# A decoder block's first MLP operands made all through the attention, loads issued further ahead at changes of stage, and w_down's sums spread over five products

## The chip, the cores and the metric

The kernel runs as one program on one core of a Trainium2 chip. The metric is the device time of one execution in microseconds (us). The profile speaks of TensorE (PE, and PEld for its weight loads), VectorE (DVE), ScalarE (ACT), GpSimd (POOL) and SyncE (SP). Two engines issue transfers here: SP, whose queue shows as SPq, and POOL. Each queue is worked off in order, so an entry that waits holds what stands behind it.

## What is computed

One layer over 2048 tokens of width 1024. The reference, cut to what matters here:

```python
h = rms_norm(x, pre_norm_mix) * (1 + sc_a) + sh_a
y = hybrid_mixer(h, ...)          # GLA heads and differential attention, concatenated, @ w_out
x = x + gt_a * rms_norm(y, post_norm_mix)

h = rms_norm(x, pre_norm_mlp) * (1 + sc_m) + sh_m
y = jnp.square(jax.nn.relu(h @ w_up)) @ w_down     # 1024 -> 4096 -> 1024
x = x + gt_m * rms_norm(y, post_norm_mlp)
```

`diff_attention` is causal, two softmax maps for each of 4 heads, with (p1 - lam * p2) @ v. All values are f32.

## The kernel before

A product of f32 accuracy is made of three matmuls: each operand is split into a high part (rounded by a copy on ACT) and a low part (the rest, a subtraction on DVE), and high*high, high*low and low*high are summed in PSUM. So an operand passes through a load, ACT and DVE before PE can use it.

The stages stand one after the other in the program: modulation and projections with GLA; attention over the first 1024 tokens (`attention((0, 1), ...)`, here A0), then over the second 1024 (A1), with the product by w_out (`out_proj`) run as filler between their steps; the rest of `out_proj`; w_up; w_down. A scheduler sets the order of instructions on each engine from the order of the code and its own model, and tiles come from pools with a fixed number of buffers, so that a load waits until the last reader of its buffer is through.

**Attention.** For a query block of 128 and a key chunk of 512, `qk` makes the scores S (PE) and moves them to SBUF with a running minimum (DVE, L214 and L217); `softmax` does the exponentials (ACT, L227) and joins the two maps (DVE, L233); two steps later `pv` transposes P (PT, PE L248), copies it out (PTs, ACT L250) and multiplies with V (O, PE L252); `finish` normalises a head's output (`don` on DVE, its transposes `dps` on PE) and stores it in `mixS`.

**out_proj.** For one token tile (128 tokens) it loads `mx` from `mixS` and `xt` from x, makes 48 matmuls (Y, L873 to L875) in 16 resumptions, adds the result to x (`wxt`, on POOL for tiles below 11), stores it in `x1S`, and stores the row-normalised tile in `xnS`. `interleave` resumes it between attention steps, as soon as the heads of a tile are finished (`ready`). Tiles 0 to 10 are done so, in this order; tiles 11 to 15 after the attention.

**First operands of w_up.** `prep_first` takes the normalised rows of the first 1024 tokens back from `xnS` (`xnq`), transposes them (`ntr`), modulates them (`hBq`, ACT), forms four differences (`hTq`, DVE) and stores seven operands in `hS[0]`. It does so in 16 groups, once 132 resumptions of `out_proj` are through, that is late in A1. Its loads are on SP's queue, its stores on POOL's.

**MLP.** w_up and w_down are 2x2 block products by the Strassen-Winograd scheme, seven products each (numbered 1 to 7, with operand slots `OP`). In w_up, for each half g of the tokens' operands and each pair of column tiles, the order of products is `WORD = (1, 6, 5, 2, 7, 3, 4)`; an operand `hhi`, `hlo` of the tokens is loaded and split by `load_op` two steps (one product of two weight tiles, 24 matmuls) before its use. Results go through `up_out` into seven sums `uS`. In w_down the order is `DORD = (1, 2, 6, 7, 4, 5, 3)`, 16 steps p each; `down_ops` loads one `us` (512 KB) and one weight tile and splits both, two steps ahead (`AHEAD`). `down_w` makes the weights' sums: in product 1 the blocks a21 + a22 - a11, stored in `wdS[p][0]`; in product 2 it loads that back and stores a12 minus it in `wdS[p][1]`; products 6 and 3 load those, 7 and 5 make a sum each. At the end, `final` adds a token tile to the residual and stores it; `load_x1` fetches that residual into four buffers.

Of the kernel before, what the change touches and what calls it, by code (L numbers as in the profile page):

```python
# [19 lines left out]
P = 128  # L20
S = 2048
D = 1024
# [27 lines left out]
def tile_hybrid_block(  # L50
# [851 lines left out]
    wdS = [dram.tile([P, 2, 512], F32, name=f"wdS{p}") for p in range(NP_)]  # L902


    def prep_first(pool, tag):


        for i in range(4):
            for k in range(4):
                raw = pool.tile([P, 2, 2, P], F32, tag="prq", name="xnq", bufs=2)  # L910
                for j in range(2):
                    nc.sync.dma_start(raw[:, j], xnS[0][:, 4 * j + i].rearrange("p (e k) c -> p e k c", e=2)[:, :, k, :])
                ps = pp.tile([P, 2, 2, P], F32, tag=tag, name="ntr", bufs=2)
                yield
                for e in range(2):
                    for j in range(2):
                        nc.tensor.transpose(ps[:, e, j, :], raw[:, j, e, :], ident)
                bt = pool.tile([P, 2, 2, P], F32, tag="prq", name="hBq", bufs=2)
                for e in range(2):
                    kk = k + 4 * e  # L920
                    nc.scalar.activation(bt[:, e], ps[:, e], AF.Identity, bias=cols[:, 24 + kk:25 + kk],
                                         scale=prem[:, 1, kk:kk + 1])
                tt = pool.tile([P, 4, P], F32, tag="prq", name="hTq", bufs=2)
                cs = slice(P * i, P * i + P)
                b4 = bt.rearrange("p i j c -> p (i j) c")
                nc.vector.tensor_tensor(tt[:, 0:2], bt[:, :, 1, :], b4[:, 0:2], op=ALU.subtract)
                nc.vector.tensor_tensor(tt[:, 2], b4[:, 3], tt[:, 0], op=ALU.subtract)
                nc.vector.tensor_tensor(tt[:, 3], b4[:, 2], tt[:, 2], op=ALU.subtract)
                nc.gpsimd.dma_start(hS[0][:, 0, k, cs], b4[:, 0])
                nc.gpsimd.dma_start(hS[0][:, 1:3, k, cs], b4[:, 2:4])  # L930
                nc.gpsimd.dma_start(hS[0][:, 3:7, k, cs], tt)
                yield
# [3 lines left out]
    op = out_proj(range(TB))  # L936

    def interleave(at, first, rate, later, pre=None):
# [3 lines left out]
        while run(at, 1):  # L942
            due += rate if i < first else later
            while due >= 1.0:
                if len(wsteps) == 16 * TB or not ready(len(wsteps) // 16):
# [34 lines left out]

    c2 = ExitStack()
# [33 lines left out]
    def load_op(g, i, pool):  # L1015

        hi = pool.tile([P, 4, 512], F32R, tag=f"hhi{i}", name="hhi", bufs=1)
        lo = pool.tile([P, 4, 512], F32R, tag=f"hlo{i}", name="hlo", bufs=1)
        for kp in range(2):
            ks = slice(2 * kp, 2 * kp + 2)  # L1020
            src = prep_tile("hsrc", [P, 2, 512])
            nc.sync.dma_start(src, hS[g][:, OP[i], ks, :])
# [41 lines left out]
    WORD = (1, 6, 5, 2, 7, 3, 4)  # L1064
# [3 lines left out]
    op = out_proj(range(TB, 16))  # L1068
    run(op, 2)
    load_op(0, 1, sh)  # L1070
    run(op, 14)
    for p in range(2):
        for w in BLOCKS:
            load_w1(p, w)
            run(op, 4)
        sums_w(p)
    run(op, 8)
# [61 lines left out]
    n = len(usteps)  # L1139
    prep_todo = [(k, hf) for k in range(4) for hf in range(2)]  # L1140
    for s, (g, c, wi, p) in enumerate(usteps):
        i = WORD[wi]
        if s + 2 < n:
            g2, c2_, wi2, p2 = usteps[s + 2]
# [22 lines left out]
        if g == 0 and c >= 1 and wi in (2, 5) and p % 2 == 0 and prep_todo:  # L1167
            prep_step(1, *prep_todo.pop(0), pp, (("ntr", 1), ("ntr", 1)))
    assert not prep_todo
# [18 lines left out]
    def wd_sum(p, at):  # L1188
        t = sd.tile([P, 512], F32, tag="wds", name="wds", bufs=4)
        nc.sync.dma_start(t, wdS[p][:, at, :])  # L1190
        return t

    def down_w(i, p):

        if i == 1:
            wt = wd_block(p, 0, 0)
            a21, a22 = wd_block(p, 0, 1, "wdx"), wd_block(p, 1, 1, "wdx")
            nc.vector.tensor_tensor(a21, a21, a22, op=ALU.add)
            nc.vector.tensor_tensor(a21, a21, wt, op=ALU.subtract)
            nc.gpsimd.dma_start(wdS[p][:, 0, :], a21)  # L1200
        elif i == 2:
            wt = wd_block(p, 1, 0)
            s2 = sd.tile([P, 512], F32, tag="wdx", name="wdx", bufs=4)
            nc.sync.dma_start(s2, wdS[p][:, 0, :])
            nc.vector.tensor_tensor(s2, wt, s2, op=ALU.subtract)
            nc.gpsimd.dma_start(wdS[p][:, 1, :], s2)
        elif i in (6, 3):
            wt = wd_sum(p, 0 if i == 6 else 1)
        elif i == 7:
            wt, a21 = wd_block(p, 0, 0), wd_block(p, 0, 1, "wdx")  # L1210
# [233 lines left out]
```

## Time and profile before

| | before |
|---|---|
| time, median of 3 executions (lowest to highest) | 2688.37 us (2684.86 to 2694.07) |
| profiled execution, its own time / span of the profile | 2693.08 us / 2691.4 us |
| PE busy, share of span | 2508.6 us, 93% |
| DVE / ACT / POOL busy | 60% / 43% / 15% |
| bytes moved | 485.08 MB, mean 180 GB/s |

The span is the profiled part of one execution; its own time has 1.7 us around it. Idle time of an engine that isn't the bottleneck costs nothing, so what counts is where PE is not at work, and for what. The stages lie in the span as follows: everything ahead of `out_proj` up to 853 us, the change from A0 to A1 at 896 to 920, A1 to about 1340, the rest of `out_proj` to 1381, w_up to 2033, w_down from 2043 to the end.

### The profile page before, as it was taken

To read this page: it belongs to the slowest core of one execution; us is meant where nothing else is said; L and a number is where in the kernel's file an instruction comes from. 1 tells how busy PE (TensorE), PEld (TensorE's weight loads), DVE (VectorE), ACT (ScalarE), POOL (GpSimd) and SP (SyncE) were. 2 spreads that over 40 slices of the span, in tenths; PEclk is the share of its full clock that TensorE was granted. 3 is DMA by queue.
4 is the path that set the end of the run, shared out by engine and by line. 5 is a ranking of instruction groups with operands and counts; after the bars stand their busy time and mean duration, and the time that the engine had idled before them with its cause. 6 is when DMAs were issued, how large, how long until landed. Compare 5 with 4: busy or idle time off the path is not lost.

```text
span 2691.4 us, 35441 instructions
## 1 busy us (share of the span) xinstructions
PE 2508.6 (93%) x12532; PEld 2058.0 (76%) x12532; DVE 1605.8 (60%) x3126; ACT 1159.0 (43%) x2185; POOL 403.3 (15%) x594
## 2 busy tenths in 40 slices
PE   3999999999998999988889999999998899999998
PEld 2887787877796788766668888788886678888886
DVE  5545855247865586767358666866665444543756
ACT  3352224312555465555436455645443324232444
POOL 1211322103311101123102222122111100000000
PEclk8999999999998999999889999999999999999999
DMA  6354551345635654555367564645337874654855
GB/s 230 103 197 132 188 184 58 131 130 191 216 126 182 207 175 166 165 175 182 128 228 236 189 232 161 207 149 172 127 128 260 296 259 143 189 167 158 269 182 193
DMA packets 224346, 485.08 MB, mean 180 GB/s; under 512 B 25456, under 2 KB 87712, under 8 KB 222624
## 3 DMA queue, kind: packets, MB, share of 16 engines
q1 hardware_dynamic: 178768, 331.17, 39.0%
q0 software_dynamic: 45392, 151.56, 15.3%
q8 instruction: 101, 1.65, 0.3%
q14 instruction: 85, 0.70, 0.1%
HBM read 327.43 MB, written 155.20 MB: 179 GB/s over the span
## 4 chain that ended last, share of the span: by engine, by line
PE 45%; issue 12%; DVE 4%; DMA 3%; POOL 3%; ACT 1%; SPq 0%; POOLq 0%; DVEq 0%; ACTq 0%
PE dn L1310 6%; PE dn L1309 6%; PE dn L1308 6%; PE upY L1163 3%; PE upY L1164 3%; PE upY L1165 3%; PE S L209 2%; PE upV L1165 2%; PE upV L1163 2%; PE upV L1164 2%; PE O L252 2%; PE upX L1163 2%; PE upX L1165 2%; PE upX L1164 2%; PE PT L248 1%
## 5 line engine op out<-in xcount | busy, mean ns | idle before, releaser
L1310 PE MATMUL dn<-dnhi,ulo 128*128 128x512 f32 x896 | 352.9, 394 | 13.2 <-DVE ulo L1235 13.1
L1308 PE MATMUL dn<-dnhi,uhi 128*128 128x512 f32 x896 | 352.2, 393 | 13.1 <-ACT dnhi L1232 10.2
L1309 PE MATMUL dn<-dnlo,uhi 128*128 128x512 f32 x896 | 351.8, 393 | 0.2 <-DVE dnlo L1234 0.2
L1233 ACT CAST uhi<-us 128x1024 fp32r<-128x1024 f32 (+1 forms) x128 | 120.7, 945 | 343.6 <-PE dn L1309 289.2
L1235 DVE TENSOR_TENSOR ulo<-us,uhi 128x1024 fp32r<-128x1024 f32 (+1 forms) x128 | 139.4, 1089 | 163.8 <-ACT uhi L1233 163.4
L1310 PEld LDWEIGHTS dn<-dnhi,ulo 128*128 128x128 f32 x896 | 169.8, 190 | 51.5 <-DVE ulo L1235 15.7
L1308 PEld LDWEIGHTS dn<-dnhi,uhi 128*128 128x128 f32 x896 | 170.0, 190 | 50.4 <-ACT dnhi L1232 10.8
L488 PE MATMUL projt<-hThi,whi 128*128 128x512 f32 x512 | 207.2, 405 | 0.6 <-DVE cols L370 0.3
L489 PE MATMUL projt<-hTlo,whi 128*128 128x512 f32 x512 | 206.6, 403 | 0.0
L490 PE MATMUL projt<-hThi,wlo 128*128 128x512 f32 x512 | 202.1, 395 | 2.1 <-DVE wlo L425 2.1
L209 PE MATMUL S<-K,q 128*128 128x512 f32 (+3 forms) x640 | 192.3, 394 | 11.2 <-DVE P L214 7.2
L1309 PEld LDWEIGHTS dn<-dnlo,uhi 128*128 128x128 f32 x896 | 170.0, 190 | 37.1 <-DVE dnlo L1234 1.0
L227 ACT ACTIVATE P<-P,nm 128x128 f32<-128x128 f32 (+15 forms) x128 | 153.7, 1202 | 63.6 <-DVE nm L217 62.9
L1055 ACT CAST wuhi<-wA 128x512 fp32r<-128x512 f32 x160 | 99.0, 619 | 167.2 <-PE upV L1164 71.9
L252 PE MATMUL O<-V,PTs 128*128 128x128 f32 x1088 | 157.2, 289 | 11.4 <-ACT PTs L250 7.3
L252 PEld LDWEIGHTS O<-V,PTs 128*128 128x128 f32 x1088 | 139.2, 197 | 35.4 <-ACT PTs L250 28.2
L1163 PE MATMUL upY<-hhi,wuhi 128*128 128x512 f32 x384 | 153.4, 400 | 11.3 <-ACT hhi L1023 11.2
L1165 PE MATMUL upY<-hhi,wulo 128*128 128x512 f32 x384 | 153.4, 399 | 2.0 <-DVE wulo L1056 2.0
L1164 PE MATMUL upY<-hlo,wuhi 128*128 128x512 f32 x384 | 153.4, 399 | 0.0
L502 PE MATMUL projn<-whi,hThi 128*128 128x256 f32 x512 | 149.1, 291 | 4.1 <-DVE cols L370 2.6
L503 PE MATMUL projn<-wlo,hThi 128*128 128x256 f32 x512 | 148.3, 290 | 0.0
L504 PE MATMUL projn<-whi,hTlo 128*128 128x256 f32 x512 | 146.8, 287 | 0.0
(309 smaller groups left out, 5684.9 us busy)
## 6 DMA issues: line engine op xcount, KB each, us to landing
us<-uS SPq DMA_DIRECT2D x96, 512.0 KB, 4.2
wA<-in_w_up_dram SPq DMA_DIRECT2D x128, 256.0 KB, 3.0
uS<-t POOLq DMA_DIRECT2D x128, 256.0 KB, 3.0
adaraw<-in_ada_w_dram SPq DMA_DIRECT2D x48, 512.0 KB, 4.3
wraw<-in_w_in_dram SPq DMA_DIRECT2D x48, 512.0 KB, 4.5
uS<-c POOLq DMA_DIRECT2D x96, 256.0 KB, 3.0
K<-kS SPq DMA_DIRECT2D x40, 512.0 KB, 4.7
wds<-in_w_down_dram SPq DMA_DIRECT2D x80, 256.0 KB, 4.5
```

What stands on the lines that cost most here:

```text
L209: nc.tensor.matmul(ps[:, :wd], qt[:, m, hl, qs], Kc[ci][:, m, :wd], start=(hl == 0), stop=(hl == 1))
L227: nc.scalar.activation(Ps[m][:, :width], Ps[m][:, :width], AF.Exp, scale=-1.0, bias=nms[m][:, t:t + 1], accum_out=sums[:, 0, m:m + 1])
L252: nc.tensor.matmul(outs[t, h][:, j, :], pt[:, kb % 4, :], Vc[g][:, kb % 4, :], start=(kb == 0), stop=(kb == nb - 1))
L488: nc.tensor.matmul(ps, whi[k][:, cs], hi[:, k, :], start=(k == 0), stop=False)
L489: nc.tensor.matmul(ps, whi[k][:, cs], lo[:, k, :], start=False, stop=False)
L490: nc.tensor.matmul(ps, wlo[k][:, cs], hi[:, k, :], start=False, stop=(k == NK - 1))
L1163: nc.tensor.matmul(ps, whi[:, k, :], hi[:, k, :], start=(first and k == 0), stop=False, skip_group_check=not first)
L1164: nc.tensor.matmul(ps, whi[:, k, :], lo[:, k, :], start=False, stop=False, skip_group_check=not first)
L1165: nc.tensor.matmul(ps, wlo[:, k, :], hi[:, k, :], start=False, stop=(k == 3), skip_group_check=not first)
L1308: nc.tensor.matmul(banks[t], uhi[:, tk], whi, start=first, stop=False, skip_group_check=on)
L1309: nc.tensor.matmul(banks[t], uhi[:, tk], wlo, start=False, stop=False, skip_group_check=on)
L1310: nc.tensor.matmul(banks[t], ulo[:, tk], whi, start=False, stop=last, skip_group_check=on)
```

## The change

- `out_proj` works through the first eight token tiles in the order 0, 4, 1, 5, 2, 6, 3, 7 (`TOKS`), since one group of `prep_first` needs tiles i and i + 4.
- `prep_first` runs from the start of the attention's second half: group n begins when the tiles that it needs are through. Its loads are on POOL's queue in place of SP's and are issued three attention yields ahead of the transposes (one before), with two yields behind a group.
- `load_op` is parted into `fetch_op` (loads) and `split_op` (ACT and DVE), three and two products ahead. The operands of products 1 and 6 lie in a pool of their own (`sq`), and those of products 1, 6 and 5 no longer wait for `out_proj`'s pool. The second token half's first operands are fetched and split in the last round of the first half.
- The operands of w_down's first two steps are loaded and split inside w_up's last round, into buffers of `sq`.
- `down_w` forms other sums at other places: a11 - a21 in product 1 or 2 (by p), a22 minus it in product 6, a12 minus that for two p in every second step of products 7 and 4, a21 + a22 in product 5. There are four subtractions or additions for each p where there were five, three stored sums where there were two. The number of matmuls stays.
- The residual has three buffers, not four, and the last tile's final sum and store come in two halves.

```diff
+    TOKS = (0, 4, 1, 5, 2, 6, 3, 7) + tuple(range(8, 16))
     def prep_first(pool, tag):
-        for i in range(4):
-            for k in range(4):
-                raw = pool.tile([P, 2, 2, P], F32, tag="prq", name="xnq", bufs=2)
-                for j in range(2):
-                    nc.sync.dma_start(raw[:, j], xnS[0][:, 4 * j + i]...[:, :, k, :])
-                ps = pp.tile([P, 2, 2, P], F32, tag=tag, name="ntr", bufs=2)
+        for n in range(16):
+            i, k = n // 4, n % 4
+            while len(wsteps) < 32 * (i + 1) + 4:
+                yield
+            raw = pool.tile([P, 2, 2, P], F32, tag="prq", name="xnq", bufs=2)
+            for j in range(2):
+                nc.gpsimd.dma_start(raw[:, j], xnS[0][:, 4 * j + i]...[:, :, k, :])
+            for _ in range(3):
+                yield
+            ps = pp.tile([P, 2, 2, P], F32, tag=tag, name="ntr", bufs=2)
...
+            for _ in range(2):
                 yield
...
-    op = out_proj(range(TB))
+    op = out_proj(TOKS[:TB])
...
-            if pre is not None and len(wsteps) >= 132:
+            if pre is not None:
                 run(pre, 1)
...
-    def load_op(g, i, pool):
-        hi = pool.tile([P, 4, 512], F32R, tag=f"hhi{i}", name="hhi", bufs=1)
-        lo = pool.tile([P, 4, 512], F32R, tag=f"hlo{i}", name="hlo", bufs=1)
+    def fetch_op(m):
+        g, i = opseq[m]
+        hsrc[m] = [prep_tile("hsrc", [P, 2, 512]) for _ in range(2)]
         for kp in range(2):
+            nc.sync.dma_start(hsrc[m][kp], hS[g][:, OP[i], 2 * kp:2 * kp + 2, :])
+    def split_op(m):
+        g, i = opseq[m]
+        ph, pl = {1: (sq, sq), 6: (sq, sh), 5: (sh, sh)}.get(i) or (sm, sm)
...
-            if c2_ == 0 and p2 % 2 == 0 and (g2, wi2) != (0, 0):
-                load_op(g2, WORD[wi2], sh if WORD[wi2] == 1 else sm)
+        if p % 2 == 0:
+            m = 7 * g + wi if c == 0 else (wi if c == NP_ // 2 - 1 and g == 0 else None)
+            for ahead, f in ((2, split_op), (3, fetch_op)):
+                if m is not None and m + ahead < 14 and (m + ahead >= 7 * (g + 1)) == (c > 0):
+                    f(m + ahead)
...
+        if (g, c, wi, p) == (1, NP_ // 2 - 1, 3, NP_ - 1):
+            wr = prep_tile("wr", [P, 2, 512])
+            ur = [prep_tile("ur", [P, 2, 512]) for _ in range(2)]
+            for d in range(2):
+                nc.sync.dma_start(ur[d], uS[d][:, OP[1]])
+                nc.sync.dma_start(wr[:, d], w_down[2 * d * P:2 * d * P + P, 0:512])
...
+        if (g, c, wi) == (1, NP_ // 2 - 1, 5):
+            d = p % 2
...
+            ready_ops[d] = (uq[:, 0:1024], uq[:, 1024:2048], wq[:, 2 * d, :], wq[:, 2 * d + 1, :])
...
     def down_w(i, p):
-        if i == 1:
-            wt = wd_block(p, 0, 0)
-            a21, a22 = wd_block(p, 0, 1, "wdx"), wd_block(p, 1, 1, "wdx")
-            nc.vector.tensor_tensor(a21, a21, a22, op=ALU.add)
-            nc.vector.tensor_tensor(a21, a21, wt, op=ALU.subtract)
-            nc.gpsimd.dma_start(wdS[p][:, 0, :], a21)
-        elif i == 2:
-            wt = wd_block(p, 1, 0)
-            s2 = sd.tile([P, 512], F32, tag="wdx", name="wdx", bufs=4)
-            nc.sync.dma_start(s2, wdS[p][:, 0, :])
-            nc.vector.tensor_tensor(s2, wt, s2, op=ALU.subtract)
-            nc.gpsimd.dma_start(wdS[p][:, 1, :], s2)
-        elif i in (6, 3):
-            wt = wd_sum(p, 0 if i == 6 else 1)
+        if i in (1, 2):
+            wt = wd_block(p, i - 1, 0)
+            if (i == 1) == (p % 2 == 1 and p > 1):
+                a11 = wt if i == 1 else wd_block(p, 0, 0, "wdx")
+                a21 = wd_block(p, 0, 1, "wdx")
+                nc.vector.tensor_tensor(a21, a11, a21, op=ALU.subtract)
+                wd_store(p, 0, a21)
+        elif i == 6:
+            wt, s3 = wd_block(p, 1, 1), wd_sum(p, 0, "wdx")
+            nc.vector.tensor_tensor(s3, wt, s3, op=ALU.subtract)
+            wd_store(p, 1, s3)
+            wt = s3
+        elif i in (7, 4):
+            wt = wd_sum(p, 0) if i == 7 else wd_block(p, 1, 1)
+            if p % 2 == 0:
+                q = p // 2 + (8 if i == 4 else 0)
+                a12, s2 = wd_block(q, 1, 0, "wdx"), wd_sum(q, 1, "wdx")
+                nc.vector.tensor_tensor(a12, a12, s2, op=ALU.subtract)
+                wd_store(q, 2, a12)
...
-    ready_ops = {s: down_ops(*dsteps[s]) for s in range(AHEAD)}
```

How this moves instructions stands here for three places. The first is PE at the change from A0 to A1. The names are those of the attention above; S with 128x512 after the last O of A0 belongs to A1. Before, between the last O of A0 and the first S of A1, stand 74 Y matmuls; the rows are the last of them and the first S:

```order
L875 MATMUL Y<-wohi,mx 128x512
L873 MATMUL Y<-wohi,mx 128x512
L874 MATMUL Y<-wolo,mx 128x512
L209 MATMUL S<-K,q 128x512 x2
L875 MATMUL Y<-wohi,mx 128x512
L873 MATMUL Y<-wohi,mx 128x512
L874 MATMUL Y<-wolo,mx 128x512
L875 MATMUL Y<-wohi,mx 128x512
```

With the change, from the last O of A0 to the first Y behind it:

```order
L252 MATMUL O<-V,PTs 128x128 x8
L269 MATMUL dps<-ident,don 128x128 x4
L209 MATMUL S<-K,q 128x512 x8
L209 MATMUL S<-K,q 128x128 x4
L209 MATMUL S<-K,q 128x512 x8
L209 MATMUL S<-K,q 128x256 x4
L209 MATMUL S<-K,q 128x512 x2
L248 MATMUL PT<-ident,P 128x128 x4
L209 MATMUL S<-K,q 128x512 x2
L248 MATMUL PT<-ident,P 128x128 x2
```

The Y matmuls have left the change from A0 to A1, since the second tile of the new order (4) belongs to the heads that finish last in A0; they stand further on, among the S of A1.

The second place is SP's queue where w_up ends and w_down begins. `wA` is a weight block of w_up, `gtg` the gate, `us` and `wds`, `wdx` are w_down's loads, and uS_14429 is uS of step p = 0. Before:

```order
L1033 DMA wA_24367<-in_w_up_dram 128x512
L1033 DMA wA_24398<-in_w_up_dram 128x512
L1179 DMA gtg<-gtS_83 128x1024
L1222 DMA us<-uS_14429 128x1024
L1185 DMA wds<-in_w_down_dram 128x512
L1185 DMA wdx<-in_w_down_dram 128x512 x2
L1222 DMA us<-uS_14430 128x1024
```

With the change:

```order
L1053 DMA wA_24370<-in_w_up_dram 128x512
L1053 DMA wA_24401<-in_w_up_dram 128x512
L1274 DMA us<-uS_14431 128x1024
L1231 DMA wds<-in_w_down_dram 128x512
L1274 DMA us<-uS_14432 128x1024
L1231 DMA wds<-in_w_down_dram 128x512
L1231 DMA wdx<-in_w_down_dram 128x512
L1274 DMA us<-uS_14433 128x1024
L1225 DMA gtg<-gtS_83 128x1024
```

The first load of w_down that stands behind w_up's is now that of step 2; those of steps 0 and 1 stand earlier, inside w_up.

The third place is SP's queue from product 1 to product 2 of w_down (wdS_14445 is wdS of p = 0, and us<-uS_14429 is step 0 of product 2). Before:

```order
L1222 DMA us<-uS_14444 128x1024
L1185 DMA wds<-in_w_down_dram 128x512
L1185 DMA wdx<-in_w_down_dram 128x512 x2
L1222 DMA us<-uS_14429 128x1024
L1185 DMA wds<-in_w_down_dram 128x512
L1204 DMA wdx<-wdS_14445 128x512
L1185 DMA wds<-in_w_down_dram 128x512
L1204 DMA wdx<-wdS_14446 128x512
L1185 DMA wds<-in_w_down_dram 128x512
L1222 DMA us<-uS_14430 128x1024
```

With the change:

```order
L1274 DMA us<-uS_14444 128x1024
L1231 DMA wds<-in_w_down_dram 128x512
L1231 DMA wdx<-in_w_down_dram 128x512 x4
L1274 DMA us<-uS_14429 128x1024
L1231 DMA wds<-in_w_down_dram 128x512
L1231 DMA wdx<-in_w_down_dram 128x512 x3
L1274 DMA us<-uS_14430 128x1024
L1231 DMA wds<-in_w_down_dram 128x512
L1231 DMA wdx<-in_w_down_dram 128x512
L1236 DMA wdx<-wdS_14445 128x512
```

Before, the loads of stored sums begin with the first step of product 2; now the loads of plain blocks for the sums of product 2 come ahead of them, most of them while product 1 still runs.

More of the change, by code (lines that the diff above doesn't have):

```diff
@@ L901, in tile_hybrid_block @@
     uS = [dram.tile([P, 7, 2, 512], F32, name=f"uS{p}") for p in range(NP_)]
-    wdS = [dram.tile([P, 2, 512], F32, name=f"wdS{p}") for p in range(NP_)]
+    wdS = [dram.tile([P, 3, 512], F32, name=f"wdS{p}") for p in range(NP_)]
+    TOKS = (0, 4, 1, 5, 2, 6, 3, 7) + tuple(range(8, 16))
     def prep_first(pool, tag):
-        for i in range(4):
-            for k in range(4):
-                raw = pool.tile([P, 2, 2, P], F32, tag="prq", name="xnq", bufs=2)
-                for j in range(2):
-                    nc.sync.dma_start(raw[:, j], xnS[0][:, 4 * j + i].rearrange("p (e k) c -> p e k c", e=2)[:, :, k, :])
-                ps = pp.tile([P, 2, 2, P], F32, tag=tag, name="ntr", bufs=2)
-                yield
-                for e in range(2):
-                    for j in range(2):
[L917 to L931, printed above, removed]
@@ new lines, in prep_first @@
+        for n in range(16):
[4 more added lines that the diff above has]
+            for j in range(2):
+                nc.gpsimd.dma_start(raw[:, j], xnS[0][:, 4 * j + i].rearrange("p (e k) c -> p e k c", e=2)[:, :, k, :])
+            for _ in range(3):
+                yield
+            ps = pp.tile([P, 2, 2, P], F32, tag=tag, name="ntr", bufs=2)
+            for e in range(2):
+                for j in range(2):
+                    nc.tensor.transpose(ps[:, e, j, :], raw[:, j, e, :], ident)
+            bt = pool.tile([P, 2, 2, P], F32, tag="prq", name="hBq", bufs=2)
+            for e in range(2):
+                kk = k + 4 * e
+                nc.scalar.activation(bt[:, e], ps[:, e], AF.Identity, bias=cols[:, 24 + kk:25 + kk],
+                                     scale=prem[:, 1, kk:kk + 1])
+            tt = pool.tile([P, 4, P], F32, tag="prq", name="hTq", bufs=2)
+            cs = slice(P * i, P * i + P)
+            b4 = bt.rearrange("p i j c -> p (i j) c")
+            nc.vector.tensor_tensor(tt[:, 0:2], bt[:, :, 1, :], b4[:, 0:2], op=ALU.subtract)
+            nc.vector.tensor_tensor(tt[:, 2], b4[:, 3], tt[:, 0], op=ALU.subtract)
+            nc.vector.tensor_tensor(tt[:, 3], b4[:, 2], tt[:, 2], op=ALU.subtract)
+            nc.gpsimd.dma_start(hS[0][:, 0, k, cs], b4[:, 0])
+            nc.gpsimd.dma_start(hS[0][:, 1:3, k, cs], b4[:, 2:4])
+            nc.gpsimd.dma_start(hS[0][:, 3:7, k, cs], tt)
+            for _ in range(2):
@@ L944, in interleave @@
             while due >= 1.0:
-                if len(wsteps) == 16 * TB or not ready(len(wsteps) // 16):
+                if len(wsteps) == 16 * TB or not ready(TOKS[len(wsteps) // 16]):
                     due = 0.0
@@ L1063, in tile_hybrid_block @@
     BLOCKS = ((1, 1), (2, 1), (2, 2), (1, 2))
-    WORD = (1, 6, 5, 2, 7, 3, 4)
     usteps = [(g, c, wi, p) for g in range(2) for c in range(NP_ // 2) for wi in range(7) for p in (2 * c, 2 * c + 1)]
-    op = out_proj(range(TB, 16))
-    run(op, 2)
-    load_op(0, 1, sh)
+    op = out_proj(TOKS[TB:])
+    fetch_op(0)
     run(op, 14)
+    split_op(0)
+    fetch_op(1)
+    run(op, 12)
     for p in range(2):
@@ L1074, in tile_hybrid_block @@
             load_w1(p, w)
-            run(op, 4)
+            run(op, 2)
+    split_op(1)
+    fetch_op(2)
+    run(op, 14)
+    for p in range(2):
         sums_w(p)
-    run(op, 8)
+        run(op, 2)
     split_w1(0, 1)
@@ L1269, in final @@
         xt, y, r = x1t.pop(ti), ya.pop(ti), fr.pop(ti)
-        nc.vector.scalar_tensor_tensor(xt, y, r, xt, op0=ALU.mult, op1=ALU.add)
-        nc.sync.dma_start(out[ti * P:(ti + 1) * P, :], xt)
+        for cs in ((slice(512, D), slice(0, 512)) if ti == NTOK - 1 else (slice(0, D),)):
+            nc.vector.scalar_tensor_tensor(xt[:, cs], y[:, cs], r, xt[:, cs], op0=ALU.mult, op1=ALU.add)
+            nc.sync.dma_start(out[ti * P:(ti + 1) * P, cs], xt[:, cs])
     def down_out(i, t):
```

46 lines of the change are left out of this document (32 added, 14 removed).

## The prediction

> **What bounds the kernel now.** I read the page's head first, then what PE waited for over the whole span, then windows around each change of stage. The two lines of the page give the span and each engine's busy time:
>
> ```profile
> span 2691.4 us, 35441 instructions
> PE 2508.6 (93%) x12532; PEld 2058.0 (76%) x12532; DVE 1605.8 (60%) x3126; ACT 1159.0 (43%) x2185; POOL 403.3 (15%) x594
> ```
>
> PE is the bound: only 183 us of the span lie outside its work, and the change leaves its matmuls as they are. So the prediction is a sum over PE's lost time. Its waits (total, times, longest), those on which the edits bear:
>
> ```profile
> PE dn L1310 <- DVE ulo L1235: 13.1, 5, 6.8
> PE ntr L917 <- DMA xnq<-xnS: 18.0, 14, 3.2
> PE upY L1163 <- ACT hhi L1023: 11.2, 1, 11.2
> PE dn L1308 <- ACT dnhi L1232: 10.2, 1, 10.2
> PE dps L269 <- DVE don L266: 6.9, 5, 5.2
> PE dn L1308 <- ACT uhi L1233: 3.0, 2, 1.8
> PE upY L1165 <- DVE wulo L1056: 2.0, 1, 2.0
> ```
>
> Then windows: the stretch and its width, busy time and count of PE, PEld, DVE, ACT and POOL, granted clock, DMA share, GB/s:
>
> ```profile
> 896.20:920.20 24.00, 20.75 (x81) 16.32 (x80) 5.84 (x19) 7.24 (x23) 5.05 (x6) 0.86 0.99 338
> 920.20:960.00 39.80, 38.09 (x228) 30.67 (x227) 34.64 (x105) 24.05 (x43) 3.49 (x3) 1.00 0.49 152
> 960.00:1150.00 190.00, 186.70 (x1083) 153.21 (x1082) 135.18 (x398) 111.31 (x228) 20.43 (x19) 0.99 0.50 161
> 1150.00:1312.00 162.00, 131.29 (x716) 104.98 (x716) 106.60 (x292) 86.03 (x163) 45.90 (x62) 0.92 0.54 169
> 1382.00:1404.00 22.00, 10.73 (x36) 7.88 (x35) 11.66 (x24) 10.14 (x22) 2.14 (x4) 0.71 0.46 164
> 1404.00:1720.00 316.00, 316.00 (x1389) 254.48 (x1388) 230.58 (x354) 175.77 (x283) 73.26 (x129) 1.00 0.62 208
> 1720.00:1731.00 11.00, 8.99 (x32) 6.66 (x31) 9.65 (x14) 7.58 (x13) 3.78 (x7) 0.84 0.81 272
> 2033.00:2048.00 15.00, 4.83 (x16) 3.46 (x15) 6.56 (x9) 4.49 (x6) 2.92 (x6) 0.66 0.95 332
> 2048.00:2116.00 68.00, 64.23 (x274) 52.10 (x273) 37.32 (x49) 17.94 (x23) 7.05 (x13) 0.97 0.85 286
> 2116.00:2165.00 49.00, 37.89 (x147) 29.98 (x147) 19.85 (x26) 15.82 (x23) 5.42 (x10) 0.90 0.88 301
> 2165.00:2660.00 495.00, 495.00 (x2178) 408.66 (x2177) 256.88 (x384) 176.76 (x293) 4.88 (x9) 1.00 0.61 196
> ```
>
> The reader is to see three things. Inside w_up and late w_down PE is full: 316.00 us for 1389 matmuls is 0.2275 us each, so a step of 24 is 5.46 us. The losses sit at the changes of stage and late in A1. And behind a wait the clock is down (0.66 to 0.90) where it is 1.00 elsewhere. So for the MLP I take as lost a window's width less its count times 0.2275, which holds both the wait and the slow matmuls behind it; a few missing records would make it a little too high.
>
> **A, first operands out of late A1.** Of the 162 us of 1150 to 1312 PE is idle 30.7, against 3.3 in the 190 us before. 18.0 of them are the waits for `xnq`, 5.2 one wait for `don`. The loads stood one yield ahead, on SP, and SP was held there by the stores of the same step:
>
> ```profile
> SPq L912 <- DMA hS<-hBq: 70.4, 18, 9.2
> SPq L912 <- DMA xnS<-wyt: 7.4, 1, 7.4
> xnq<-xnS SPq DMA_DIRECT2D x32, 128.0 KB, 3.0
> hS<-hBq POOLq DMA_DIRECT2D x16, 128.0 KB, 2.3
> ```
>
> Now they stand three yields ahead. A1 yields 120 times (its steps counted in the code) in the 392 us from 920 to 1312, every 3.3 us, so three are 9.8 us against a landing of 3.0: the waits go, if POOL issues in time. The 16 groups still issue 64 transposes, four differences, and all their loads and stores; they move from the end of A1 to its first two thirds, where the other engines have room (DVE 135.18 of 190). I take −16 for A: 18.0 and about 3 for the clock after them (mean 0.92 over the window), less 5 for new waits of this kind at the fuller place. Ends: 0 and −23. The `don` wait (5.2): in the new order that `dps` stands among Y matmuls that used to be spent at 896; −4, ends 0 and −5. The moved loads and stores also pass `wxt` and `xnS` on POOL's queue, and small waits of S and PT for them among the steps cost +2 (0 to +5).
>
> **B, the change from A0 to A1.** Here the move takes cover away. The 74 Y matmuls that filled it:
>
> ```profile
> 896.20:920.10 23.90, 20.21 (x74) 15.72 (x74) 1.41 (x2) 2.07 (x6) 0.86 1.00 340
> 886.65 0.69 SPq L185 DMA_DIRECT2D K<-kS  x1
> 893.98 10.42 SPq L197 DMA_DIRECT2D q<-qS  x8
> q<-qS SPq DMA_DIRECT2D x9, 128.0 KB, 8.0
> 920.20 0.62 PE L209 MATMUL S<-K,q 128*128 128x512 f32 x2
> 931.43 0.63 PE L248 MATMUL PT<-ident,P 128*128 128x128 f32 x4 [0.69 <-DVE P L233]
> ```
>
> Those 74 take 74 × 0.2275 = 16.8 us and four `dps` 0.6, so before 24.0 − 17.4 = 6.6 us were lost. With the change PE has only `dps` and S from 896. The first q is issued at 893.98 and lands 8.0 us later, so S can begin near 902 to 903: 6.8 us idle. From the first S to the first PT are 11.2 us, in which the 26 S matmuls that stand there take about 6: 5.2 idle, and 1.7 for the clock behind it. Before, Y filled that ramp too (38.09 busy of 39.80, so at most 1.7 lost). Net 6.8 + 5.2 + 1.7 − 6.6 = +7. Ends: S at 898 and half the ramp hidden, −2; S not before 912, when the last of the eight q has landed (904.4 + 8.0), +16. The Y matmuls themselves are not saved: they stand among later steps and take the same time there.
>
> **C, loads ahead in the MLP.** Where the stages change:
>
> ```profile
> 1398.58 1.22 PE L1163 MATMUL upY<-hhi,wuhi 128*128 128x512 f32 x2 [11.24 <-ACT hhi L1023]
> 2037.62 0.33 SPq L1222 DMA_DIRECT2D us<-uS  x1
> 2043.44 1.65 PE L1308 MATMUL dn<-dnhi,uhi 128*128 128x512 f32 x3 [10.17 <-ACT dnhi L1232]
> us<-uS SPq DMA_DIRECT2D x96, 512.0 KB, 4.2
> ```
>
> - Into w_up: 22.00 − 36 × 0.2275 = 13.8 lost. The operands of products 1, 6 and 5 no longer wait for `out_proj`'s pool, so loads and splits lie beside its last matmuls. −13 (ends −14, −6 if the first weight's split is late instead).
> - Change of g: 11.00 − 32 × 0.2275 = 3.7. −3 (0 to −3.7); the splits now run in the round before, on ACT and DVE with 283 and 354 instructions in 316 us.
> - Into w_down: 15.00 − 16 × 0.2275 = 11.4. Two steps are now ready, 10.9 us of PE work. SP's first load for step 2 stands where step 0's did, at 2037.62; from there to the first matmul it took 5.8 us, so step 2 is ready near 2043.5, and PE, which stopped at 2033.3, reaches it at 2044.2. That is just enough; I keep 1.4 for a miss: −10 (ends −11.4, −5).
>
> [...]
>
> **D, w_down's sums.** Lost in products 1 and 2: 68.00 − 274 × 0.2275 = 5.7, and 49.00 − 147 × 0.2275 = 15.6, which hold the waits for `ulo` and `uhi`. A step of product 1 before loads 512 KB of `us` and three blocks of 256 KB and stores one: 1.57 MB in 5.46 us is 288 GB/s, and these windows ran at 286 and 301. So DMA bounds that stretch, not PE, and SP stood behind buffers:
>
> ```profile
> SPq L1204 <- DMA wdS<-wdx: 45.2, 12, 8.4
> SPq L1185 <- DMA wdS<-wdx: 51.4, 11, 7.2
> wdx<-in_w_down_dram SPq DMA_DIRECT2D x64, 256.0 KB, 4.3
> wdS<-wdx POOLq DMA_DIRECT2D x32, 256.0 KB, 3.4
> ```
>
> With the change products 1 and 2 have one sum in two steps or so, 1.05 to 1.2 MB a step, some 195 to 220 GB/s, as in the full stretch 2165 to 2660 (196). −4 (0 to −5.7) and −14 (−6 to −15.6). What is given back: in the new order on SP the loads of all 16 sums a12 − s2 are drawn together into about 12.5 steps of product 7. A sum holds one of four `wdx` buffers for load 4.3, the sum and store 3.4, about 8.4 us, and another one for the loads; two at a time is 4.2 us a sum, 67 us for 16, where 12.5 steps are 68. That is at its limit: +3 (0 to +12).
>
> **E, the end.** Three residual buffers may hold the last loads behind a store, the halves let the last store start half a sum earlier: 0 (−0.5 to +1).
>
> **Sum.** −16 − 4 + 2 + 7 − 13 − 3 − 10 − 4 − 14 + 3 = −52. The profiled execution took 2693.08, so 2641; it lies 4.7 above the median of 2688.37, and against that I say 2636. About 0.3% (8 us) is what can be told from no change here.
>
> **Rivals.**
>
> Attention gives nothing (0.18): loads that come late on POOL take the old waits' place, so A is 0 and B +7 to +16. The rest, −39, then leaves −32 to −23: 2656 to 2665. For it: POOL's queue held `wxt` for long before, and the moved loads pass it. Against it: three yields are 9.8 us, and POOL's own transfers of 128 KB landed in 2.3 us where SP's took 3.0, with DVE at work for 106.60 of 162 us. [...]
>
> Sums jam in product 7 (0.15): 0.79 MB of operands a step and 16/12.5 sums of 0.79 are 1.80 MB, 330 GB/s, near the 338 and 332 of the densest windows. If only the 286 of product 1 are had, 68 us become 78: +10 in place of +3, and some 4 more where the loads for the sums of product 2 crowd into the end of product 1: 2643 to 2650. Against it: windows with a DMA share of 0.95 to 0.99 show that the rate exists.
>
> w_down's first operands are not early (0.04), because their buffers come free late and the edit does nothing: the last term of C is 0, 2646.
>
> Slower (0.06): SP's hold passes to POOL. A load there waits for its buffer, and behind it stand the addition `wxt` and the stores; ACT waits for `wxt`, and behind ACT's wait stand the exponentials and PTs that PE needs. POOL's and ACT's waits of that kind before, the first of the whole span, the second of 925 to 1310:
>
> ```profile
> POOL wxt L888 <- DVE wyt L886: 121.7, 9, 30.6
> ACT wyt L892 <- POOL wxt L888: 8.1, 6, 2.8
> ```
>
> The hold on SP was 70.4 + 7.4 = 77.8 us. Without A's gain the time is 2656, so the hold decides for slower if more than 40 us of it, about half, reach PE; all of it would give 2734. Against it: POOL was waiting for DVE 121.7 us in that row, so it has slack, and little of its lateness reached ACT.
>
> **How the numbers follow.** The forecast that all parts act has 0.57, and its own range from the terms' ends, not all at once, is 2616 to 2656. The rivals have 0.18, 0.15, 0.04 and 0.06. The range reaches up over the first two to 2670 and down to 2612, where A and D give nearly their ends (all ends together would be about 2607). Slower by over 0.3% (above 2696) has the last rival's 0.06; within it 0.08, from the first rival with some of that hold besides; faster 0.86, from the others.
>
> **What would show it.** Right: PE's wait for `xnq` falls from 18.0 to under 5, and the transposes `ntr` lie before 1150; PE's waits for `hhi`, `dnhi` and `wulo` at the three changes are gone, with a clock near 1.00; the waits for `ulo` fall under 3. At the change from A0 to A1 a new idle stretch of about 7 us and a ramp with gaps appear; there the term is too small if S begins after 905. Wrong: PE's waits for PTs, P and `dps` in A1 grow by over 10 us and POOL's for its loads by as much (first and last rival); waits for `ulo` or `dnhi` in product 7, with DMA at 0.9 or more there (second); a first `us` load of step 0 that lands after w_up's last matmul (third). What I can't see from before is how long POOL's queue holds with the new entries, and that makes the prediction wrong first.

## The result, and the profile after

The changed kernel took 2620.3 us, median of four executions (2618.5 to 2620.5), against 2690.5 for the kernel before (2684.9 to 2694.1, four): the ratio is 0.974, 95% interval 0.972 to 0.976. It is 70 us faster, where 52 was forecast; 2620 lies in the range given, 2612 to 2670, near its lower end. One execution of the run below with product 6's operand in the late pool took 4855.5 us, in a slow state, and is left out of its figures. The two lines of the page that answer to those shown of before:

```profile
span 2618.7 us, 35437 instructions
PE 2482.6 (95%) x12532; PEld 2043.2 (78%) x12532; DVE 1595.4 (61%) x3111; ACT 1154.8 (44%) x2185; POOL 435.5 (17%) x642
```

The span is 72.7 us shorter, with the same 12532 matmuls. 26.0 of that is PE's own busy time: the same matmuls took less of it, at a higher granted clock (0.96, 0.99 and 0.98 in the three windows of before below, 0.97, 1.00 and 0.99 after). The rest is waiting. PE's waits after, those that answer to the list of before:

```profile
PE Y L873 <- DMA mx<-mixS: 11.4, 2, 7.1
PE dps L269 <- DVE don L266: 5.2, 3, 4.2
PE dn L1361 <- DVE du L1339: 4.7, 1, 4.7
PE upX L1195 <- DVE wulo L1076: 3.4, 3, 1.7
PE upY L1195 <- DVE wulo L1076: 1.5, 1, 1.5
PE ntr L923 <- DMA xnq<-xnS: 1.2, 1, 1.2
```

The 18.0 us for `xnq` are 1.2, and the waits for `hhi`, `dnhi`, `uhi` and `ulo` have left the list. New are a wait for `du` and one of 4.3 us for `mx` late in `out_proj`; the 7.1 for `mx` stand at the first Y, where before 7.0 stood for PTs. Where the 72.7 us are is read from three windows in each kernel: from the first Y to the first upX, w_up, and w_down with the end. Before, then after (columns as in the prediction's windows):

```profile
852.95:1381.65 528.70, 484.43 (x2704) 395.94 (x2705) 334.51 (x948) 279.94 (x574) 85.32 (x104) 0.96 0.56 181
1381.65:2033.27 651.62, 638.33 (x2752) 513.17 (x2752) 448.79 (x698) 342.83 (x563) 137.07 (x247) 0.99 0.52 176
2033.27:2691.40 658.13, 621.33 (x2688) 508.96 (x2688) 339.00 (x507) 225.34 (x370) 20.04 (x37) 0.98 0.65 214
```

```profile
851.09:1354.84 503.75, 476.06 (x2705) 390.08 (x2706) 340.50 (x955) 284.31 (x585) 108.79 (x137) 0.97 0.60 195
1354.84:1989.03 634.19, 629.33 (x2754) 510.19 (x2753) 445.01 (x692) 339.00 (x557) 135.47 (x245) 1.00 0.53 182
1989.03:2618.70 629.67, 614.83 (x2689) 505.28 (x2687) 325.67 (x490) 221.33 (x366) 29.17 (x54) 0.99 0.69 228
```

Attention and `out_proj` are 25.0 us shorter, w_up 17.4, w_down 28.5; the stretch ahead of them, whose code is the same, is 1.9 shorter. In the attention PE's busy time fell by 8.4 us for the same matmuls, its idle time by 16.6 (44.3 to 27.7).

In w_down each product has 384 matmuls, 87.0 us when PE is full. Products 1 and 2 before, then products 1, 2, 6 and 7 after:

```profile
2043.44:2143.30 99.86, 92.93 (x384) 75.04 (x385) 54.05 (x71) 31.75 (x43) 10.84 (x20) 0.95 0.88 298
2143.30:2241.30 98.00, 90.04 (x386) 73.67 (x386) 41.39 (x51) 29.62 (x45) 6.50 (x12) 0.97 0.71 238
```

```profile
1988.87:2076.70 87.83, 87.45 (x386) 71.95 (x385) 43.27 (x55) 30.91 (x44) 11.87 (x22) 1.00 0.88 309
2076.70:2163.70 87.00, 87.00 (x385) 72.04 (x384) 33.95 (x40) 29.51 (x45) 3.78 (x7) 1.00 0.63 204
2163.70:2255.60 91.90, 87.22 (x386) 71.93 (x384) 43.77 (x57) 31.39 (x48) 8.65 (x16) 0.99 0.74 247
2255.60:2344.90 89.30, 89.28 (x384) 73.29 (x385) 42.45 (x54) 23.61 (x31) 4.87 (x9) 0.98 0.69 233
```

Lost before: 12.9 + 11.0 = 23.9 us. After: 0.8 and 0 there, but 4.9 + 2.3 = 7.2 in products 6 and 7, where nothing was lost before. What happens there stands in the order of time, just ahead of product 7 (start, length, engine and line, operation, the idle time before it and what ended it). Three rows are DVE's; the second is SP's, the issue of the load that the third row waits for:

```profile
2249.86 0.69 DVE L1261 TENSOR_TENSOR wdx<-wdx 128x512 f32<-128x512 f32 x1 [1.87 <-DMA wdx<-wdS]
2250.88 0.32 SPq L1236 DMA_DIRECT2D wdx<-wdS  x1
2254.15 0.69 DVE L1261 TENSOR_TENSOR wdx<-wdx 128x512 f32<-128x512 f32 x1 [3.59 <-DMA wdx<-wdS]
2254.76 0.68 DVE L1339 TENSOR_TENSOR du<-dp,dn 128x512 f32<-128x512 f32 x1
```

`du` takes product 6's result out of PSUM, and the first matmul of product 7 waited 4.7 us for it. PE was through at 2250.9. DVE stood until 2254.15 behind a sum for a later product, whose load hadn't landed; only then came `du`, and PE went on at 2255.6. The load itself was no slower than others: 3.3 us from its issue to the sum, where such loads take 4.2 (median). It was issued late, since SP had waited 3.2 us for a store out of a `wdx` buffer.

### The profile page after: what moved, and what is told of

It reads as the page before. It is cut to its first block, busy times and chain, and to the rows that moved or that the text cites. A ratio compares the mean times of both kernels' runs of the same rounds, so it can differ in the third digit from the quotient of the medians.

```text
span 2618.7 us, 35437 instructions
## 1 busy us (share of the span) xinstructions
PE 2482.6 (95%) x12532; PEld 2043.2 (78%) x12532; DVE 1595.4 (61%) x3111; ACT 1154.8 (44%) x2185; POOL 435.5 (17%) x642
## 4 chain that ended last, share of the span: by engine, by line
PE 33%; issue 20%; DMA 5%; POOL 5%; DVE 3%; ACT 2%; SPq 0%; POOLq 0%; DVEq 0%; ACTq 0%
PE dn L1361 6%; PE dn L1363 6%; PE dn L1362 6%; PE O L252 3%; PE S L209 3%; PE Y L873 1%; PE Y L875 1%; POOL uS L1121 1%; PE Y L874 1%; POOL uS L1152 1%; PE PT L248 1%; DMA mx<-mixS 1%; PE upY L1195 1%; PE upY L1194 1%; PE upY L1193 1%
## 5 line engine op out<-in xcount | busy, mean ns | idle before, releaser
L1361 PE MATMUL dn<-dnhi,uhi 128*128 128x512 f32 x880 | 344.2, 391 | 4.8 <-DVE du L1339 4.7
L1363 PE MATMUL dn<-dnhi,ulo 128*128 128x512 f32 x880 | 343.8, 391 | 0.1
L1362 PE MATMUL dn<-dnlo,uhi 128*128 128x512 f32 x880 | 343.8, 391 | 0.0
L209 PEld LDWEIGHTS S<-K,q 128*128 128x128 f32 x640 | 111.7, 197 | 48.8 <-DVE P L214 21.9
```

What stands on the lines that cost most here:

```text
L209: nc.tensor.matmul(ps[:, :wd], qt[:, m, hl, qs], Kc[ci][:, m, :wd], start=(hl == 0), stop=(hl == 1))
L1361: nc.tensor.matmul(banks[t], uhi[:, tk], whi, start=first, stop=False, skip_group_check=on)
L1362: nc.tensor.matmul(banks[t], uhi[:, tk], wlo, start=False, stop=False, skip_group_check=on)
L1363: nc.tensor.matmul(banks[t], ulo[:, tk], whi, start=False, stop=last, skip_group_check=on)
```

## Experiments: the attention

A word on noise. The kernel before has medians from 2684 to 2690 us beside the runs below, and the changed kernel has 2620.3 here and 2624.1 when measured again. In seven profiles with the same code in the attention, the stage from the first Y to the first upX takes 500.1 to 508.4 us, 503.7 in the middle. So a few us in a total, or in one profile of a stage, say little.

**The attention part undone.** Tiles in their own order, `prep_first` late, with its loads on SP and one yield ahead:

```diff
-    TOKS = (0, 4, 1, 5, 2, 6, 3, 7) + tuple(range(8, 16))
+    TOKS = tuple(range(16))
-            if pre is not None:
+            if pre is not None and len(wsteps) >= 132:
+    (prep_first as in the kernel before)
```

> The changed kernel with its attention part undone: tiles of out_proj in their own order, prep_first as before (after 132 resumptions, loads on SP, one yield ahead). The MLP keeps all of the change. Theory (the attention part is worth by itself what its stage shows, 25 us from the first Y to the first upX): 2620 + 25 = 2645 us, PE waits for xnq again some 18 us in 14 waits, and PE's busy time for the same matmuls of that stage about 8 us more because the granted clock is low behind the waits. Rival (part of the 25 us comes from the MLP's earlier loads, which now find SP's queue free at the end of the attention): under 2637 us, with the stage less than 17 us longer. Second rival (late operands of product 1 now hold w_up, since its fetches stand earlier): over 2652 us with a wait at the first upX or upY.

Measured: 2653.65 us (2647.1 to 2661.7), ratio to before 0.988 (0.985 to 0.991). The stage is back at its old length, and so are the waits (the second row is SP's, in 1100 to 1330):

```profile
848.90:1381.25 532.35, 483.98 (x2705) 396.66 (x2705) 340.20 (x956) 284.99 (x583) 85.37 (x105) 0.95 0.57 186
PE ntr L920 <- DMA xnq<-xnS: 17.4, 13, 3.1
SPq L915 <- DMA hS<-hBq: 67.4, 17, 9.1
```

28.6 us longer than with the change, 7.9 of it busy time, where the theory had 25 and 8. The first rival falls. The total is 33 over, so over the 2652 of the second rival too, but its sign is missing: at the start of w_up PE waits 1.9 us in all. What is left over lies in w_down, whose code is the same: it took 627 from its first to its last matmul in this profile and 620 in that of the changed kernel, with waits of 3.1 us for `ulo` and 2.0 for `c` that the latter doesn't have or has at 0.4. Why they came, the runs don't show.

**Late, but nothing to load.** Is it the late place that costs, or the loads there? This kernel leaves out the loads, so that the operands of w_up's first half aren't the layer's; the other work stays.

```diff
-                raw = pool.tile([P, 2, 2, P], F32, tag="prq", name="xnq", bufs=2)
-                for j in range(2):
-                    nc.sync.dma_start(raw[:, j], xnS[0][...])
-                        nc.tensor.transpose(ps[:, e, j, :], raw[:, j, e, :], ident)
+                        nc.tensor.transpose(ps[:, e, j, :], ident, ident)
```

> The run with the attention part undone, but prep_first loads nothing: its transposes take the identity matrix, so the operands of w_up's first half are wrong numbers; all transposes, copies, differences and stores stay at the late place. Theory (in the late place what cost was the wait for loads that can't be issued early, because their buffers wait for a store to land): the 28 us of that stage come back nearly whole, 2612 to 2624 us, although the groups stand as late and as dense as before. Rival (the place costs: groups crowd PE, ACT and DVE late in the attention, and the clock falls with short gaps): at most 10 of the 28 us come back, 2640 us or more. In between, both.

Measured: 2631.28 us (2624.9 to 2635.2), 22 below the run before. In its profile (the execution of 2624.9) the stage is this:

```profile
851.89:1357.70 505.81, 476.26 (x2705) 390.98 (x2705) 336.21 (x952) 283.16 (x582) 84.97 (x104) 0.97 0.56 186
```

26.5 of the 28.6 us are back, busy time included, with the groups as late as before and denser: the transposes stand from 1146.9 to 1254.4, where in the run before they stood from 1145.9 to 1295.3. So it was the loads, not the crowd. The median is above the 2612 to 2624 that I expected, so between 22 and 26 us hang on the loads. The edit takes away three things at once: PE's wait for `xnq`, SP's hold, and one of the three tiles of a group that share two buffers. It doesn't part them.

**One yield ahead in place of three**, at the early place:

```diff
-            for _ in range(3):
-                yield
+            yield
...
-            for _ in range(2):
+            for _ in range(4):
                 yield
```

> The changed kernel with prep_first's loads one yield ahead of the transposes in place of three (four yields behind a group in place of two, so the groups keep their distance and place). Theory (three yields of lead cover the landing; one, about 3.3 us, does not cover a landing of 3 us and the queue): waits for xnq on PE come back at the early place, 10 us or more of the former 18, with slow clock: 2632 to 2640 us. Rival (the waits came from SP being held by the stores of the step before; on POOL and with groups further apart nothing holds the load): under 3 us of waits for xnq, 2618 to 2624 us.

Measured: 2631.8 us (2630.3 to 2639.7), ratio 0.980 (0.978 to 0.982), 11 over the changed kernel. The stage and the wait:

```profile
859.35:1372.73 513.38, 476.18 (x2705) 388.68 (x2706) 334.79 (x954) 281.12 (x582) 108.61 (x137) 0.97 0.58 192
PE ntr L922 <- DMA xnq<-xnS: 6.2, 7, 2.0
```

The theory holds in the total's sign and falls short in the wait: 6.2 us where 10 or more were expected, and the stage 9.6 longer. This is the profile of the slowest of the four executions (2639.7), but its stage is also 5 us longer than the longest with three yields. Lead is worth some 5 to 10 us even with the groups far apart.

**Loads on SP.**

```diff
-                nc.gpsimd.dma_start(raw[:, j], xnS[0][...])
+                nc.sync.dma_start(raw[:, j], xnS[0][...])
```

> The changed kernel with prep_first's loads on SP's queue, as before, place and lead as in the change. Theory (queue): SP is held there again by buffers whose last reader is a store, and the K, V and q of the attention behind it come late: PE waits of 5 us or more for xnq and for K or q, 2626 to 2640 us. Rival (with three yields of lead and groups five yields apart the queue doesn't matter): 2618 to 2624 us.

Measured: 2617.07 us (2613.8 to 2619.2), ratio 0.974 (0.972 to 0.977), the same as the change; no wait for `xnq` is among PE's. The rival is right: given the lead, the queue doesn't matter. SP was held as long as in the run with the attention part undone (900 to 1345):

```profile
SPq L917 <- DMA hS<-hBq: 67.9, 17, 10.8
```

The hold came without a wait on PE, and the stage took 501.0 us. So of the things that the run without loads took away together, SP's hold by itself, at the early place and with the lead, cost nothing. Whether three yields of lead would have done at the late place too was not run.

**Tiles in their own order**, the groups as early as that allows:

```diff
-    TOKS = (0, 4, 1, 5, 2, 6, 3, 7) + tuple(range(8, 16))
+    TOKS = tuple(range(16))
-            while len(wsteps) < 32 * (i + 1) + 4:
+            while len(wsteps) < 16 * (i + 5) + 4:
```

> The changed kernel with out_proj's tiles in their own order 0 to 7; a group of prep_first begins when its two tiles are through, so the first needs five tiles and the last eight. Theory: 74 Y matmuls fill the change from A0 to A1 again (4 to 5 us gained there), but the groups can't start before the fifth tile and crowd later, with waits for xnq of up to 5 us: within 2616 to 2628 us. Rival (the order of the tiles is what takes the operands out of the late part): as with the attention part undone, 2640 us or more. Second rival (the hole costs as much as was forecast, 7 us, and the order is needed for nothing): 2613 us or less.

Measured: 2617.1 us (2614.7 to 2623.1), ratio 0.975 (0.973 to 0.978). The stage:

```profile
850.86:1349.51 498.65, 469.25 (x2704) 386.55 (x2705) 339.19 (x957) 285.46 (x587) 108.72 (x137) 0.98 0.60 198
```

It is 5.1 us shorter than with the new order in the changed kernel's profile, as the theory had it, and 1.5 shorter than the shortest of the seven; in the total that can't be told from the change. So the new order of the tiles isn't needed, and the hole that it leaves from A0 to A1 costs some 2 to 6.

## Experiments: w_up

**One product ahead**, as before, with the change's pools:

```diff
-            for ahead, f in ((2, split_op), (3, fetch_op)):
+            for ahead, f in ((1, fetch_op), (1, split_op)):
...
-    fetch_op(1)
...
-    split_op(1)
-    fetch_op(2)
```

> The changed kernel with w_up's operands fetched and split one product ahead, as before, the pools as in the change. Theory (the lead is what removes the waits): the wait at the first matmul of product 6 comes back, up to 11 us, and that at the change of g, 2 us, with their slow clock: +12 to +17, 2632 to 2637 us. Rival (the pool was the hindrance: loads waited for out_proj's buffers, and with buffers of their own one product of lead, 11 us, is enough): +0 to +4, at most 2624 us.

Measured: 2621.04 us (2619.1 to 2622.3), ratio 0.9755 (0.9735 to 0.9774): no difference. The theory falls as far as the place in the code goes. The scheduler moved the loads and copies of product 6 up by itself, its copies to 1338.9, ahead of w_up's first matmul at 1353.0, so the lead itself was not taken away.

**Product 6's operand in the late pool besides.**

```diff
-        ph, pl = {1: (sq, sq), 6: (sq, sh), 5: (sh, sh)}.get(i) or (sm, sm)
+        ph, pl = {1: (sq, sq), 5: (sq, sh)}.get(i) or (sm, sm)
```

> As the run with w_up's operands one product ahead, and product 6's operand besides in the pool that takes out_proj's place (product 5's stays outside it). To be compared with that run. Theory (where the buffers lie decides when the loads can be issued): the wait of about 11 us for hhi at the first matmul of product 6 is back: +11 to +14 over it, 2632 to 2636 us. Rival (the loads' place on SP's queue and prep_first's early end removed the wait): within 3 us of it.

Measured: 2629.5 us (2629.1 to 2634.5, three executions), ratio 0.980 (0.9775 to 0.983), 8 over the run before; in the profiles w_up up to w_down's first matmul is 13.0 us longer (648.2 against 635.2). PE's wait, and ACT's copy that it waits for:

```profile
PE upY L1190 <- ACT hhi L1043: 11.9, 1, 11.9
1363.81 1.99 ACT L1043 CAST hhi<-hsrc 128x1024 fp32r<-128x1024 f32 x2 [4.62 <-DMA xnS<-wyt]
```

The wait of before, 11.24 us, is back. The second row says why: the copy's target lies where `out_proj` had its tiles, and waits until the last of them is stored in `xnS`. So with the code's lead the same in both runs, the place of the buffers decides.

## Experiments: w_down

**First operands after w_up.** The early loads and splits are taken out, and in their place:

```diff
-    assert len(ready_ops) == AHEAD
+    ready_ops = {s: down_ops(*dsteps[s]) for s in range(AHEAD)}
```

> The changed kernel without w_down's first operands inside w_up; steps 0 and 1 are loaded and split after it, as before. Theory: a wait for dnhi of about 10 us at the first dn matmul and half the clock behind it: +11 to +13, 2631 to 2633 us. Rival (the early operands also gave the queue a lead that removes waits in the rest of product 1): +17 or more, with new waits for ulo or uhi in the first 70 us of w_down.

Measured: 2634.67 us (2626.7 to 2641.0), ratio 0.980 (0.977 to 0.983), 14 over the change. PE's waits, and product 1:

```profile
PE dn L1345 <- ACT dnhi L1268: 3.8, 1, 3.8
PE dn L1346 <- DVE dnlo L1270: 3.2, 1, 3.2
1997.27:2091.20 93.93, 90.32 (x384) 73.63 (x385) 44.24 (x55) 31.18 (x43) 9.22 (x17) 0.95 0.85 295
```

In w_down the size is about the theory's: 3.8 us of waiting ahead of product 1 and 6.9 lost in it make 10.7, where 11 to 13 were expected. Both waits belong to step 0: the second stands at 2002.1, after its first three matmuls, and the matmuls behind it start 0.43 us apart, not 0.23. From 2005 to 2090 PE waits only 0.4 us, so the rival, that the early operands give the whole product a lead, falls. The rest of the 14 isn't w_down's: in this profile the stage of the attention, whose code is the same, is 4.7 longer than in the changed kernel's.

**And the old sums** (`wd_sum` and `down_w` as in the kernel before), to be compared with that run:

> As the run without w_down's early first operands, and down_w's sums of before besides (a21 + a22 - a11 in product 1, a12 minus it in product 2, two stored sums). To be compared with that run. Theory (the sums' load on DMA and buffers in products 1 and 2 cost 5.7 + 15.6 = 21 us, and the new places give back 6.7 at the change from product 6 to 7): 21 - 7 = +14 to +15 over it, the waits for ulo back at the change from product 1 to 2, and the wait for du at the change from 6 to 7 gone. Rival (the waits in products 1 and 2 followed from the late start of w_down): those are in both runs, so +5 or less. Second rival (the wait for du at 6 to 7 is of w_down's own): it stays, +21.

Measured: 2642.66 us (2637.2 to 2657.1), 8 over the run without early operands, in ranges that overlap. Products 1, 2 and 6, and the wait:

```profile
1994.79:2097.40 102.61, 93.60 (x384) 75.30 (x385) 57.77 (x75) 31.96 (x43) 11.93 (x22) 0.93 0.90 309
2097.40:2189.80 92.40, 89.01 (x386) 73.18 (x385) 38.79 (x48) 29.59 (x45) 5.96 (x11) 0.98 0.69 230
2189.80:2276.80 87.00, 87.00 (x385) 72.06 (x384) 39.52 (x49) 29.82 (x47) 0.00 (x0) 1.00 0.51 161
PE dn L1341 <- DVE ulo L1265: 9.9, 4, 3.4
```

Products 1 and 2 lose 15.6 + 5.4 = 21.0, and the wait for `du` is gone: it came with the new sums. That this is the theory's 21 is chance, since 6.9 of it, at step 0, were in the run to compare with too. The old sums by themselves bring 14 there, not 21, and after what they give back about 6: from its first to its last matmul w_down takes 632.8 us here and 626.6 in that run. The theory's +14 to +15 isn't met, its two signs are, and the rival's +5 isn't parted from this.

**A version that gives less back.** One edit of the changed kernel:

```diff
-                a12, s2 = wd_block(q, 1, 0, "wdx"), wd_sum(q, 1, "wdx")
+                a12, s2 = wd_block(q, 1, 0, "wdx"), wd_sum(q, 1)
```

> The changed kernel with one edit: the stored sum that product 7 and 4 load for a12 - s2 goes into the buffers of the weights (wds) in place of wdx, so these loads keep the order of the steps and the sums stand one in two steps over products 7 and 4, not 16 in 12 steps. Theory (DVE stood behind a sum that waited for its load when the banks of product 6 had to be copied out, 4.7 us and the clock behind it, 7 us in products 6 and 7 together): -4 to -7 against the changed kernel in this call. Rival (the sum that stands ahead of the copies waits just as long, since SP is in order and wds has only four buffers): within 2 us, or slower by waits for ulo or dnlo in product 7.

> The changed kernel itself, for comparison on the same chip: 2616 to 2623 us, ratio to before 0.974 as measured first.

Measured: 2614.78 us (2610.0 to 2617.9) against 2624.14 (2612.7 to 2627.2) for the changed kernel, which lies a little above the 2616 to 2623 expected; ratios to before 0.974 (0.972 to 0.976) and 0.976 (0.973 to 0.979). Products 6 and 7, and the wait for `du`:

```profile
2159.40:2246.50 87.10, 87.10 (x386) 72.11 (x385) 44.13 (x57) 29.92 (x47) 6.49 (x12) 1.00 0.71 235
2246.50:2334.10 87.60, 87.18 (x386) 71.89 (x384) 34.53 (x44) 25.73 (x33) 4.33 (x8) 1.00 0.61 197
PE dn L1361 <- DVE du L1339: 1.1, 2, 0.7
```

0.7 us are lost where 7.2 were. `wds` is taken in the order of the steps, so a load for a later sum can't run ahead of them. The wait for `du` varies: in ten profiles with the new sums its longest is 2.7 to 6.6 us (2.7 in that of the changed kernel measured again); with this edit it is 0.7, here and in the next run. From its first to its last matmul w_down takes 614.1 us, against 618.5 for the changed kernel measured again and 618.5 to 626.9 in all nine with the same code there. By the medians of the totals it is 9 us faster; the ranges and intervals overlap, so I call the mechanism shown and its worth in the total, some 4 to 8 us, likely.

With the tiles in their own order besides:

> The edit of the run before and the tiles of out_proj in their own order with groups as early as that allows. Theory (the change from A0 to A1 is filled again, 5 us in that stage, and the two edits don't touch each other): -8 to -12 against the changed kernel in this call. Rival (the gain of the tiles' order is within the noise from chip to chip, its total stood at 2617.1 against 2620.3 elsewhere): as the run before, within 2 us.

Measured: 2615.1 us (2609.4 to 2618.8). The stage is 497.88 (500.8 without it), but the total is the same: the rival is right, and so small a gain can't be told here.

## Why the prediction was right, point by point

The range, the sign and most places were right; the sum was 18 to 21 us short (against the median and the profile), 14 of it in the attention.

- **A, first operands: mis-sized.** A, `don`, the small waits and B were to make −16 − 4 + 2 + 7 = −11; the stage gave −25.0. Two sizes failed, which make 9 of the 14 us; what is left lies with B, `don` and the small waits, and isn't parted. I put 5 us of new waits for `xnq` at the early place: 1.2. And I took 3 us for the slow clock behind the waits: PE's busy time fell by 8.4, and by 7.7 between the runs with late loads and with none (the wait of 5.2 for `don` went there too). The mechanism, lead against landing, held: loads gone, 22 to 26 us back; one yield, 5 to 10 us lost. POOL's queue, on which I said the prediction would fail first, did no harm that is seen, and SP served as well, held for 67.9 us.
- **`don`: wrong in place.** I said that the wait would be covered by Y. The late one went, but another of 4.2 us stands at the change from A0 to A1, ahead of the first S. So −1, not −4.
- **B, the hole: near in size, wrong in its parts.** +7 was forecast, some 2 to 6 measured by putting the tiles back. S didn't wait for q, as I had it: q was issued at 884.76, not 893.98, and S began at 897.1 behind that `dps`. Nor was the ramp up to the first PT idle time: of its 12.7 us PE idled 1.3, where I had 5.2, and the matmuls took 11.4 at a granted clock of 0.53, where I had about 6 and 1.7 for the clock. That these parts came near the size was luck.

```profile
884.76 10.29 SPq L197 DMA_DIRECT2D q<-qS  x8
896.73 0.63 PE L269 MATMUL dps<-ident,don 128*128 128x128 f32 x4 [4.19 <-DVE don L266]
897.10:909.80 12.70, 11.38 (x29) 6.37 (x27) 9.23 (x28) 4.68 (x7) 2.23 (x4) 0.53 0.82 271
909.84 1.09 PE L248 MATMUL PT<-ident,P 128*128 128x128 f32 x4 [0.20 <-DVE P L233]
```

- **C, w_up: right.** −13 − 3 = −16 against −17.4, and for the reason given, the buffers outside `out_proj`'s pool: with product 6's back inside, w_up is 13.0 longer. What the lead by itself is worth no run shows, as the scheduler kept it.
- **C and D, w_down: right in sum, not in parts.** −10 − 4 − 14 + 3 = −25 against −28.5 with the end. The gain in products 1 and 2 was −18 by my windows, −23 measured; of that the runs assign 14 to the sums, and the other 9 aren't parted. The jam was +3, and 7.2 measured. D's working of it was right: sums that take turns with four buffers need 4.2 us each, and the seven from 2228.2 to 2254.15 stand 4.3 apart. What I left out is that they stand in DVE's order ahead of `du`, so that the wait of one falls on PE. The second rival, loads too dense for DMA, is half right: the jam came, about where it said, but at a DMA share of 0.74 in product 6 and 0.69 in product 7, with a load that landed in the usual time.
- **E, the end: right**, from 10.2 us behind the last matmul to 9.6.
- **The other rivals fell.** PE's waits in the attention didn't move to POOL's queue, and w_down's first operands were early.

## What to carry to other kernels

When an operand is late, ask first what keeps its load or its copy from being issued. At the start of w_up it was a pool in the place of the stage before, whose last store had to land (11.2 us of waiting before, 11.9 with product 6's operand back in it); once the buffers lay elsewhere, the scheduler did the moving ahead by itself. In the attention loads behind a buffer whose last reader was a store needed a few steps of lead (6.2 us of waits with one yield, 1.2 with three), and with that a queue that was held for 67.9 us did no harm. And a sum made ahead of need must not stand, on the engine that also empties PSUM, between a finished product and the operation that takes it out: PE waited 4.7 us for `du` so, and at most 0.7 once the sums' loads kept the order of the steps.

## What the runs showed of the hardware

Where PE had short waits the granted clock was lower, and I had taken too little for that: 3 us, where PE's busy time in the attention's stage fell by 8.4 for the same matmuls. A stretch of the run with the attention part undone, in which PE's longest wait is 3.1 us (17.4 us for `xnq` in 13 waits, 6.3 for others), and one of the kernel before with a single wait of 1.3 us for `xnq`:

```profile
1143.00:1298.00 155.00, 130.27 (x711) 104.50 (x709) 101.42 (x282) 81.88 (x151) 43.74 (x58) 0.93 0.54 171
```

```profile
1186.00:1196.00 10.00, 8.69 (x52) 7.04 (x52) 5.82 (x17) 3.36 (x7) 4.07 (x7) 1.00 0.43 131
```

The first has a mean clock of 0.93, where 960 to 1150 of the kernel before had 0.99; the second has 1.00. The prediction's window 1720 to 1731, with one wait of 2.0 us and no other, has 0.84, where 1404 to 1720 had 1.00. So in these rows the clock was lower with a single wait of 2.0 us, and not with one of 1.3. What a wait between those lengths does, and what waits that stand close together add, these rows don't show.
